# First stage in a written order, score banks for layer 1, context squares on two engines, adaLN rows a step behind, and common buffers for the spatial weights

## The chip, the core and the metric

The kernel runs on one core of a Trainium2 chip. A core has TensorE (PE) for matrix products, VectorE (DVE), ScalarE (ACT) and GpSimd (POOL) for everything else, SyncE (SP) that issues the DMA transfers, a software-managed SBUF and the accumulator memory PSUM. The metric is the time of one launch on the device in microseconds; smaller is better. Each engine runs its own list of instructions in order and waits at semaphores for the others.

## What is computed

A two-layer diffusion backbone. 512 latent tokens and 256 context tokens of width 1024 share the weights; layer 0 is a spatial-gating MLP beside differential attention, layer 1 multi-head latent attention. Each layer starts with an RMS norm whose scale and shift come from a conditioning vector (adaLN):

```python
def reference(x, c, ctx, c_ctx, ...):
    h_lat, h_ctx = x, ctx
    for li in range(DEPTH):
        shift_l, scale_l, gate_l = adaln_terms(c, ada_w[li], ada_b[li])      # silu(c) @ w_ada + b_ada
        shift_c, scale_c, gate_c = adaln_terms(c_ctx, ada_w[li], ada_b[li])
        xl = rms_norm(h_lat, norm_w[li]) * (1.0 + scale_l[:, None, :]) + shift_l[:, None, :]
        xc = rms_norm(h_ctx, norm_w[li]) * (1.0 + scale_c) + shift_c
        out_l, out_c = even_mixer(xl, xc, ...) if li % 2 == 0 else odd_mixer(xl, xc, ...)
        h_lat = h_lat + gate_l[:, None, :] * out_l
        if li < DEPTH - 1:
            h_ctx = h_ctx + gate_c * out_c
    return rms_norm(h_lat, final_w)

def spatial_gating(u, v, w_s, b_s, ln_w, ln_b):       # half of even_mixer
    vn = layer_norm(v, ln_w, ln_b)
    vc = vn.reshape(bsz, length // 128, 128, 8, 64)
    mixed = jnp.einsum('gpq,bnqgd->bnpgd', w_s, vc) + b_s.T[None, None, :, :, None]
    return u * mixed.reshape(bsz, length, 512)
```

## The kernel before

The 768 tokens are six tiles of 128: tiles 0 to 3 are latent, 4 and 5 context. The width of 1024 is cut into four quarters of two slices of 128. Every float32 operand of a product is split into a high part (ACT rounds it, `wh` or `xh`) and a low part (a subtraction, `wl` or `xl`), and a product is three matmuls (`mm3`, L79 to L81): high by high, low by high, high by low. Weights come by `load_w`: SP loads 512 KB into one of two `raw` buffers (tile `wr`), ACT makes `wh` (L66), DVE or POOL subtracts (`wl`, L67); the results lie in three common buffers each, or in a stage's own pool, where they are named `wo` (eight buffers in pool `p_a`). PSUM has eight banks: two `mm`, two `tr` for transposes, and two `S` tiles of two banks each for attention scores, which the first stage uses as accumulators, so that its six (`avb`) are two `mm` and four `S` banks.

The order of instructions on each engine is set by the Tile framework's own scheduler from the order in the program, priorities and dependences; `tc.issue_after` holds instructions back until another is issued, and `in_order(engines)` fixes the written order of those engines.

The places that the change touches:

- First stage (L169 to L436). DVE and ACT square the tokens (`ssq_vector`, tile `jk`, L345; `ssq_quarter`, tile `junk`, L228), `rstd_of` gives 1/rms (POOL, L155), `normalise` scales the tokens in place on ACT (L362). `ada_chunk(0, 0)` multiplies the conditioning vector by one 512-column chunk of adaLN weights on PE (32 small matmuls in four groups, L175, with three idling matmuls `turn_over` (L399) between the groups), copies the row out of PSUM (`arow`, L183), transposes it (L185), and adds biases (`AD`, `gT`, L192 to L195). `modulate_in` transposes a quarter's slice (L371), writes `xh` on ACT (L374), `xm` on DVE (L376) and `xl` as their difference (L379). `av_part` then runs the first projection over the quarters as they come, first four tiles of latents, then the two of context. Chunk 1 of the adaLN (L175 again) follows in the same stage.
- adaLN in the later stages: `ada_step` is called between the groups of matmuls of a projection and does one `ada_chunk`, with the row copied by ACT (L181).
- Spatial stage (L479 to L487): the weights `wsT` are split into `p_a`'s `wo` buffers, as are those of the az columns behind it. For each of eight groups PE makes three matmuls into an `mm` bank, and DVE evicts it (tile `au`, L486). Next come the az columns (az0, az1), then the query and key columns (q0, k0, ...), whose weights use the common buffers.
- Output projection of layer 0 and input of layer 1: the weights `owa` (four chunks of 448 columns) are split with the subtraction on POOL.
- Layer 1: `rows_done` transposes K' (L778) and the rotary key (L782) through `tr` banks; `latent_queries` accumulates in an `mm` bank; `odd_out` makes the output columns of each token tile in `mm` banks, adds them to the residual (`y` L1009, `xr` L1010), squares on ACT (L1012) and multiplies by the final weight (`yt`, L1013), on POOL for the first two quarters. After the last quarter of a tile `rstd_of` (L232, L234, POOL L155) and a scaling end it.

Of the kernel before, what the change touches and what calls it, by code (L numbers as in the profile page):

```python
# [30 lines left out]
def tile_backbone(ctx: ExitStack, tc: tile.TileContext, a: dict, out: bass.AP):  # L31
# [137 lines left out]
    def ada_chunk(li, j, ws, between=None, copy=None):  # L169


        ps = tr_ps()
        for kt in range(8):
            for b in range(4):
                PE.matmul(ps[32 * b:32 * b + 32, :P], c32[:, kt, :], ws[kt // 2][:, kt % 2, b * P:(b + 1) * P],  # L175
                          start=kt == 0, stop=kt == 7)
            if between and kt % 2:
                between(3)
        row = til(p_bg, [P, P], F32, "arow", 2)
        if copy is ACT:  # L180
            ACT.activation(row, ps[:, :P], AF.Copy)  # L181
        else:
            DVE.tensor_copy(row, ps[:, :P])  # L183
        ps = tr_ps()
        PE.transpose(ps[:, :P], row, ident)  # L185
        r = ps[:, :P].rearrange("p (b v) -> p b v", b=4)[:, :, :2]

        def wide(x):
            n = x.shape[1]
            return x.unsqueeze(2).to_broadcast([P, n, 2])  # L190
        if j < 4:
            DVE.tensor_tensor(AD[:, li, j, :2, :], r[:, :2], wide(adab[:, li, j, :2]), op=ALU.add)  # L192
# [16 lines left out]

    def ada_step():  # L210
# [141 lines left out]
    marks = []  # L352
    rs = [rstd_of(acc, 0, 4, marks)]
    POOL.tensor_scalar(adab1, adab[:, :, :4, 2:], 1.0, None, op0=ALU.add)
    with tc.issue_after(marks[1]):
        ws_in = [split_w(w0)]

    def normalise(j, v):
        t0, n = ((0, 4), (4, 2))[v]
        for t in range(n):  # L360
            x_ = xq[j][:, t0 + t, :]
            ACT.activation(x_, x_, AF.Copy, scale=rs[v][:, t:t + 1])  # L362

    def modulate_in(j, v, i, xh, xl):
# [4 lines left out]
        ps = tr_ps()[:, :n * P]  # L369
        for t in range(n):  # L370
            PE.transpose(ps[:, t * P:(t + 1) * P], xq[j][:, t0 + t, i * P:(i + 1) * P], ident)  # L371
# [24 lines left out]
    def turn_over(n):  # L396

        for _ in range(n):
            PE.matmul(avb[5][:, :P], ident, ident, start=True, stop=True)  # L399
# [8 lines left out]


    turn_over(32)  # L410
    normalise(0, 0)
    ada_chunk(0, 0, adaw[0], between=turn_over)
    for i in range(2):
        h = modulate_in(0, 0, i, *XT[0])
    turn_over(4)
    with tc.issue_after(h.ins):
        for q in range(4):
            ssq_quarter(xq[q], acc, q, 4, 1)
            ssq_vector(q, 5)
        rs.append(rstd_of(acc, 4, 2))  # L420
        normalise(0, 1)
    for i in range(2):
        modulate_in(0, 1, i, *XT[0])
    for j in range(4):
        if j < 3:
            with tc.issue_after(h.ins):
                for v in range(2):
                    normalise(j + 1, v)
        w = [x.rearrange("p (k n) -> p k n", k=2) for x in ws_in[j]]
        av_part(j, w, range(4))  # L430
# [48 lines left out]
    wsh, wsl = (x.rearrange("p (g n) -> p g n", g=8) for x in load_w(a["wsT"], p_a, 8))  # L479
# [207 lines left out]
    for c in range(4):  # L687
# [3 lines left out]
        split(raw, h, l, eng=POOL)  # L691
# [49 lines left out]
    def rows_done(v):  # L741
# [34 lines left out]
        ps = tr_ps()  # L776
# [3 lines left out]
        ps = tr_ps()  # L780
# [94 lines left out]
    def latent_queries(h):  # L875
        ps = mm_ps()
# [121 lines left out]
    def odd_out(j, w, ts):  # L998
        c = slice(j * 256, (j + 1) * 256)
        for t in ts:  # L1000
            ps = mm_ps()[:, :256]
# [11 lines left out]
            (POOL if j < 2 else DVE).tensor_tensor(yt[t][:, c], x_, finw[:, c], op=ALU.mult)  # L1013
# [101 lines left out]
```

## Time and profile before

| | |
|---|---|
| median of three runs | 712.65 us (711.88 to 713.12) |
| profiled execution, its own time | 712.08 us |
| span of the profiled execution | 710.3 us |
| mean granted TensorE clock | 0.992 of full speed |
| PE busy | 692.3 us (97%) |
| DVE / ACT / POOL busy | 441.2 (62%) / 363.1 (51%) / 42.8 us (6%) |
| DMA | 68.89 MB, mean 97 GB/s |

The span is from the first to the last recorded instruction; the profiled execution's own time is 1.8 us longer. An engine counts as busy while one of its instructions runs, not while it waits. "Idle before" in a row of the timeline is the engine's idle time just ahead of the instruction, and the name behind the arrow is what it waited for last.

### The profile page before, as it was taken

How to read it: one execution, taken by the hardware profiler on the slowest of the kernel's cores; microseconds unless marked ns; L12 is line 12 of the kernel's file. 1: busy time of each engine (PE TensorE's matmuls, PEld its weight loads, DVE VectorE, ACT ScalarE, POOL GpSimd, SP SyncE). 2: the span in 40 equal slices, each digit the busy share in tenths (PEclk: the TensorE clock that was granted, in tenths of full speed). 3: DMA queues.
4: the chain of work that ended last, by engine and by line, in shares of the span. 5: the costliest groups of instructions: out<-in, count | busy, mean ns of one | idle time of the engine just before them, and what ended most of it. 6: DMA issues, size and time to landing. Idle time of an engine off the chain costs nothing.

```text
span 710.3 us, 12674 instructions
## 1 busy us (share of the span) xinstructions
PE 692.3 (97%) x5260; PEld 637.4 (90%) x5260; DVE 441.2 (62%) x815; ACT 363.1 (51%) x704; POOL 42.8 (6%) x45
## 2 busy tenths in 40 slices
PE   8899999999999999999999999999999999999996
PEld 7688997998998989889899999978789999999995
DVE  2556814205397883979685327676448898876754
ACT  4756223214366763666543314444348777887422
POOL 1000000121001000010000300110000000000110
PEclk9999999999999999999999999999999999999998
DMA  9944893301111011110513310150210212011402
GB/s 340 408 135 154 327 352 134 119 1 31 37 54 41 20 60 42 38 41 1 230 44 117 102 30 1 60 202 31 95 60 0 69 59 83 30 60 30 119 31 90
DMA packets 20075, 68.89 MB, mean 97 GB/s; under 512 B 3121, under 2 KB 3249, under 8 KB 20017
## 3 DMA queue, kind: packets, MB, share of 16 engines
q1 hardware_dynamic: 20016, 68.08, 27.1%
q8 instruction: 41, 0.67, 0.4%
q14 instruction: 18, 0.14, 0.1%
HBM read 65.98 MB, written 2.10 MB: 96 GB/s over the span
## 4 chain that ended last, share of the span: by engine, by line
PE 82%; DVE 7%; DMA 5%; ACT 4%; issue 1%; POOL 1%; SPq 0%; POOLq 0%; ACTq 0%
PE mm L79 18%; PE mm L81 17%; PE mm L80 17%; PE S L79 3%; PE S L80 3%; PE S L81 3%; PE tr L925 3%; DMA x<-in_x 2%; PE S L565 2%; PE S L567 2%; PE tr L583 2%; PE tr L175 1%; PE S L903 1%; PE S L907 1%; DMA wr<-in_wsT 1%
## 5 line engine op out<-in xcount | busy, mean ns | idle before, releaser
L80 PE MATMUL mm<-xl,wh 128*128 128x512 f32 (+1 forms) x240 | 84.8, 354 | 0.0
L81 PE MATMUL mm<-xh,wl 128*128 128x512 f32 (+1 forms) x240 | 84.3, 351 | 0.0
L79 PE MATMUL mm<-xh,wh 128*128 128x512 f32 (+1 forms) x240 | 84.2, 351 | 0.0
L333 ACT ACTIVATE e<-S,s 128x768 f32<-128x768 f32 (+1 forms) x80 | 65.3, 817 | 17.5 <-DVE s L332 17.1
L66 ACT ACTIVATE wh<-wr 128x1024 fp32r<-128x1024 f32 (+1 forms) x40 | 41.8, 1049 | 54.4 <-PE mm L80 21.3
L67 DVE TENSOR_TENSOR wl<-wr,wh 128x1024 fp32r<-128x1024 f32 x36 | 44.5, 1238 | 40.4 <-ACT wh L66 40.4
L332 DVE TENSOR_REDUCE s<-S 128x1 f32<-128x768 f32 (+1 forms) x80 | 67.2, 841 | 3.7 <-PE S L907 1.8
L66 ACT ACTIVATE ah<-tr 128x512 fp32r<-128x512 f32 x76 | 43.9, 596 | 24.7 <-PE tr L583 12.6
L67 DVE TENSOR_TENSOR al<-tr,ah 128x512 fp32r<-128x512 f32 x76 | 50.3, 684 | 7.8 <-ACT ah L66 6.7
L80 PE MATMUL mm<-wl,xh 128*128 128x256 f32 (+1 forms) x176 | 51.4, 292 | 0.5 <-POOL wl L67 0.5
L79 PE MATMUL mm<-wh,xh 128*128 128x256 f32 (+1 forms) x176 | 51.5, 292 | 0.0
L81 PE MATMUL mm<-wh,xl 128*128 128x256 f32 (+1 forms) x176 | 50.8, 290 | 0.0
L79 PEld LDWEIGHTS mm<-xh,wh 128*128 128x128 f32 x240 | 45.2, 188 | 5.2 <-ACT wh L66 0.2
L80 PEld LDWEIGHTS mm<-xl,wh 128*128 128x128 f32 x240 | 45.2, 188 | 4.8
L81 PEld LDWEIGHTS mm<-xh,wl 128*128 128x128 f32 x240 | 45.2, 188 | 4.7
L79 PE MATMUL mm<-wo,xh 128*128 128x256 f32 x144 | 41.2, 286 | 2.1 <-DVE au L486 2.1
L80 PE MATMUL mm<-wo,xh 128*128 128x256 f32 x144 | 40.9, 284 | 0.0
L81 PE MATMUL mm<-wo,xl 128*128 128x256 f32 x144 | 40.7, 283 | 0.0
L155 POOL TENSOR_TENSOR s<-s,mhalf 128x6 f32<-128x6 f32 (+4 forms) x15 | 16.0, 1072 | 309.8 <-DVE s L605 179.3
L80 PEld LDWEIGHTS mm<-wl,xh 128*128 128x128 f32 x176 | 33.3, 189 | 1.2 <-POOL wl L67 0.7
L79 PEld LDWEIGHTS mm<-wh,xh 128*128 128x128 f32 x176 | 33.3, 189 | 0.9 <-issue 0.4
L81 PEld LDWEIGHTS mm<-wh,xl 128*128 128x128 f32 x176 | 33.1, 188 | 0.8
(283 smaller groups left out, 2007.8 us busy)
## 6 DMA issues: line engine op xcount, KB each, us to landing
ada<-in_ada SPq DMA_DIRECT2D x40, 512.0 KB, 7.3
wr<-in_ew SPq DMA_DIRECT2D x28, 512.0 KB, 3.5
wr<-in_ewo SPq DMA_DIRECT2D x8, 512.0 KB, 3.5
wr<-in_owz SPq DMA_DIRECT2D x8, 512.0 KB, 3.5
wr<-in_adr SPq DMA_DIRECT2D x8, 512.0 KB, 3.4
wr<-in_owo SPq DMA_DIRECT2D x8, 512.0 KB, 3.7
xr<-in_x SPq DMA_DIRECT2D x4, 768.0 KB, 6.5
x<-in_x SPq DMA_DIRECT2D x4, 512.0 KB, 4.8
```

Of the source, the lines that this page charges most:

```text
L66: ACT.activation(h, src, AF.Copy)
L67: (eng or DVE).tensor_tensor(l, src, h.bitcast(F32), op=ALU.subtract)
L79: PE.matmul(ps, lh, rh, start=first, stop=False)
L80: PE.matmul(ps, lh, rl, start=False, stop=False)
L81: PE.matmul(ps, ll, rh, start=False, stop=last)
L155: return POOL.tensor_tensor(dst, src, mhalf[:, :n], op=ALU.pow)
L332: mx = DVE.tensor_reduce(nmx[:, :1], v[:, :, :w], axis=AX.XY, op=ALU.max, negate=True)
L333: ACT.activation(e.rearrange("p (c k) -> p c k", k=w), v[:, :, :w], AF.Exp, bias=nmx[:, :1], scale=1.0, accum_out=sm[:, col:col + 1])
L565: PE.matmul(S[:, c, :n], QS[:, m, qs], KS[:, m, k0:k0 + n], start=True, stop=False)
L567: scored = PE.matmul(S[:, c, :n], QS[:, m, qs], KL[:, m, k0:k0 + n], start=False, stop=True)
L583: PE.transpose(ps[:, i * 256 + q * P:i * 256 + (q + 1) * P], es[q][:, (2 * j + i) * P:(2 * j + i + 1) * P], ident)
L925: PE.transpose(ps[:, i * 256 + q * P:i * 256 + (q + 1) * P], es[q][:, (2 * j + i) * P:(2 * j + i + 1) * P], ident)
```

## The change

1. First stage. ACT, DVE and PE run in written order from `normalise(0, 0)` to the first context rows. Behind the first two groups of ada products stand two idling matmuls each, behind the third and fourth the transposes of the first quarter's two slices (into an idle accumulator bank and a `tr` bank). The first weight chunk `w0` is split inside this order: `wh` on ACT before `xh`, `wl` on DVE between the first slice's `xm` and its `xl`. The row copy `arow` stands on DVE right behind the products. Of the eight context squares ACT makes five and DVE three, where each made four. `av_first` runs the first quarter's 24 latent matmuls in three passes, high by high, low weights, low tokens.
2. `ada_chunk` is cut into `ada_products` and `ada_rows`; `ada_step` first transposes the row of the step before, then makes its own products.
3. `wsT` goes to the common `wh` and `wl` buffers.
4. `owa`'s subtractions move from POOL to DVE. K' and the rotary key are transposed into the two banks of an `S` tile, the first head's latent query goes into an `S` bank, and `odd_out` alternates between `mm` and `S` banks.
5. The final weight's multiply is on DVE for all quarters; three of the four sums of squares are added and scaled before the last quarter, and the fourth is added by one instruction behind it.

The diff, cut to its core:

```diff
-    def ada_chunk(li, j, ws, between=None, copy=None):
+    def ada_products(ws, between=None, copy=None):
...
             if between and kt % 2:
-                between(3)
+                between(kt)
...
+    def ada_rows(li, j, row):
         ps = tr_ps()
         PE.transpose(ps[:, :P], row, ident)
...
     def ada_step():
+        if ada_row:
+            ada_rows(*ada_row.pop())
         if ada_done[0] < len(ada_rest):
-            ada_chunk(*ada_loaded[ada_done[0]], copy=ACT)
+            li, j, ws = ada_loaded[ada_done[0]]
+            ada_row.append((li, j, ada_products(ws, copy=ACT)))
...
+    def av_first(w, ts):
+        (xh, xl), (wh, wl) = XT[0], w
+        for n, (x_, w_) in enumerate(((xh, wh), (xh, wl), (xl, wh))):
+            for i in range(2):
+                for t in ts:
+                    PE.matmul(avb[t], x_[:, i, t * P:(t + 1) * P], w_[:, i, :], start=n + i == 0, stop=False)
...
     turn_over(32)
-    normalise(0, 0)
-    ada_chunk(0, 0, adaw[0], between=turn_over)
-    for i in range(2):
-        h = modulate_in(0, 0, i, *XT[0])
-    turn_over(4)
-    with tc.issue_after(h.ins):
+    with in_order(ACT, DVE, PE):
+        normalise(0, 0)
+        xt0 = []
+        def fill_in(kt):
+            if kt < 5:
+                turn_over(2)
+            else:
+                i = len(xt0)
+                xt0.append(turned(0, 0, i, tr_ps() if i else avb[4]))
+        ada_chunk(0, 0, adaw[0], between=fill_in)
+        ACT.activation(w0h, w0, AF.Copy)
+        turn_over(6)
+        modulate_in(0, 0, 0, *XT[0], ps=xt0[0],
+                    between=lambda: DVE.tensor_tensor(w0l, w0, w0h.bitcast(F32), op=ALU.subtract))
+        for q in range(1, 4):
+            ssq_vector(q, 5)
+        modulate_in(0, 0, 1, *XT[0], ps=xt0[1])
         for q in range(4):
-            ssq_quarter(xq[q], acc, q, 4, 1)
-            ssq_vector(q, 5)
+            ssq_quarter(xq[q], acc, q, 4, 1 if q else 2)
         rs.append(rstd_of(acc, 4, 2))
-        normalise(0, 1)
+        normalise(1, 0)
+        h = normalise(0, 1)
+    av_first(w, range(4))
...
-    wsh, wsl = (x.rearrange("p (g n) -> p g n", g=8) for x in load_w(a["wsT"], p_a, 8))
+    wsh, wsl = (x.rearrange("p (g n) -> p g n", g=8) for x in load_w(a["wsT"]))
...
-        split(raw, h, l, eng=POOL)
+        split(raw, h, l)
...
-        ps = tr_ps()
+        S = ps_s.tile([P, 2, 512], F32, tag="S", name=nm("S"))
+        ps = S[:, 0, :]
...
-        ps = tr_ps()
+        ps = S[:, 1, :]
...
-        ps = mm_ps()
+        ps = mm_ps() if h else ps_s.tile([P, 2, 512], F32, tag="S", name=nm("S"))[:, 0, :]
...
-            ps = mm_ps()[:, :256]
+            ps = (mm_ps() if t % 2 else ps_s.tile([P, 2, 512], F32, tag="S", name=nm("S"))[:, 0, :])[:, :256]
...
-            (POOL if j < 2 else DVE).tensor_tensor(yt[t][:, c], x_, finw[:, c], op=ALU.mult)
+            DVE.tensor_tensor(yt[t][:, c], x_, finw[:, c], op=ALU.mult)
...
-        rs = rstd_of(acc, t, 1)
+        DVE.tensor_reduce(part[:, :1], acc[:, t * 4:t * 4 + 3], axis=AX.X, op=ALU.add)
+        DVE.tensor_scalar(part[:, :1], part[:, :1], 1.0 / D, 1e-6, op0=ALU.mult, op1=ALU.add)
+        odd_out(3, wo[2], (t,))
+        DVE.scalar_tensor_tensor(ms[:, :1], acc[:, t * 4 + 3:t * 4 + 4], 1.0 / D, part[:, :1], op0=ALU.mult, op1=ALU.add)
+        rsqrt(rs[:, :1], ms[:, :1], 1)
```

Where this puts the instructions is seen in the engines' lists. DVE in the first stage, before, from the first context square to the first `xm` (x_96 to x_99 are the quarters of the tokens, tr and S are PSUM banks, wr_116 is the raw chunk `w0`):

```order
L345 SCALAR_TENSOR_TENSOR jk_311,s_144<-x_96 128x256
L67 TENSOR_TENSOR wl_184<-wr_116,wh_183 128x1024
L345 SCALAR_TENSOR_TENSOR jk_315,s_144<-x_97 128x256
L345 SCALAR_TENSOR_TENSOR jk_319,s_144<-x_98 128x256
L345 SCALAR_TENSOR_TENSOR jk_323,s_144<-x_99 128x256
L183 COPY arow_280<-tr_235 128x128
L192 TENSOR_TENSOR AD<-tr_282,adab_sb 128x4
L194 TENSOR_TENSOR gT<-tr_282,adab_143 128x4
L195 TENSOR_TENSOR gT<-gT,normw_sb 128x4
L376 TENSOR_SCALAR xm_292<-tr_287,gT,AD 128x512
```

The same place in the changed kernel:

```order
L182 COPY arow_279<-tr_233 128x128
L195 TENSOR_TENSOR AD<-tr_281,adab_sb 128x4
L197 TENSOR_TENSOR gT<-tr_281,adab_143 128x4
L198 TENSOR_TENSOR gT<-gT,normw_sb 128x4
L392 TENSOR_SCALAR xm_293<-S_186,gT,AD 128x512
L452 TENSOR_TENSOR wl_196<-wr_116,wh_195 128x1024
L397 TENSOR_TENSOR xl_39_188<-xm_293,xh_38_187 128x512
L357 SCALAR_TENSOR_TENSOR jk_298,s_144<-x_97 128x256
L357 SCALAR_TENSOR_TENSOR jk_300,s_144<-x_98 128x256
L357 SCALAR_TENSOR_TENSOR jk_302,s_144<-x_99 128x256
L392 TENSOR_SCALAR xm_304<-tr_274,gT,AD 128x512
L397 TENSOR_TENSOR xl_39_188<-xm_304,xh_38_187 128x512
```

The row copy and what hangs on it now stand ahead of the squares and of `wl`, and `wl` stands between the first slice's `xm` and `xl`.

PE in the first stage, before, from the third group of ada products to the first matmuls of the projection:

```order
L175 MATMUL tr_235<-ada_112,c_14_138 32x128 x8
L399 MATMUL S_190<-ident 128x128 x3
L175 MATMUL tr_235<-ada_114,c_14_138 32x128 x8
L399 MATMUL S_190<-ident 128x128 x3
L185 MATMUL tr_282<-ident,arow_280 128x128
L371 MATMUL tr_287<-ident,x_96 128x128 x4
L371 MATMUL tr_296<-ident,x_96 128x128 x4
L399 MATMUL S_190<-ident 128x128 x4
L79 MATMUL mm_187<-wh_183,xh_40_191 128x512
L80 MATMUL mm_187<-wl_184,xh_40_191 128x512
L79 MATMUL mm_188<-wh_183,xh_40_191 128x512
L80 MATMUL mm_188<-wl_184,xh_40_191 128x512
```

The same place in the changed kernel:

```order
L174 MATMUL tr_233<-ada_112,c_14_138 32x128 x8
L378 MATMUL S_186<-ident,x_96 128x128 x4
L174 MATMUL tr_233<-ada_114,c_14_138 32x128 x8
L378 MATMUL tr_274<-ident,x_96 128x128 x4
L188 MATMUL tr_281<-ident,arow_279 128x128
L417 MATMUL S_185<-ident 128x128 x6
L433 MATMUL mm_183<-wh_195,xh_38_187 128x512
L433 MATMUL mm_184<-wh_195,xh_38_187 128x512
L433 MATMUL S_185<-wh_195,xh_38_187 128x512 x2
L433 MATMUL mm_183<-wh_195,xh_38_187 128x512
L433 MATMUL mm_184<-wh_195,xh_38_187 128x512
L433 MATMUL S_185<-wh_195,xh_38_187 128x512 x2
```

The token transposes moved ahead of the row's transpose, two of the idling groups became those transposes, and the high weights come for all four tiles before the low ones.

DVE in the spatial stage, before, from the fourth eviction (`au`) to the weights behind the last (wl_1858 is q0's, wo_1673 az1's, wl_1932 k0's):

```order
L486 SCALAR_TENSOR_TENSOR au_856<-mm_1471,absT_sb,au_856 128x6x64
L486 SCALAR_TENSOR_TENSOR au_857<-mm_1476,absT_sb,au_857 128x6x64
L486 SCALAR_TENSOR_TENSOR au_857<-mm_1481,absT_sb,au_857 128x6x64
L67 TENSOR_TENSOR wl_1858<-wr_1855,wh_1857 128x1024
L486 SCALAR_TENSOR_TENSOR au_857<-mm_1486,absT_sb,au_857 128x6x64
L486 SCALAR_TENSOR_TENSOR au_857<-mm_1491,absT_sb,au_857 128x6x64
L67 TENSOR_TENSOR wo_1673<-wr_1670,wo_1672 128x1024
L67 TENSOR_TENSOR wl_1932<-wr_1929,wh_1931 128x1024
```

The same place in the changed kernel (wl_1851 is q0's, wl_1925 k0's):

```order
L530 SCALAR_TENSOR_TENSOR au_849<-mm_1459,absT_sb,au_849 128x6x64
L198 TENSOR_TENSOR gT<-gT,normw_sb 128x4
L67 TENSOR_TENSOR wl_1851<-wr_1848,wh_1850 128x1024
L530 SCALAR_TENSOR_TENSOR au_850<-mm_1464,absT_sb,au_850 128x6x64
L530 SCALAR_TENSOR_TENSOR au_850<-mm_1469,absT_sb,au_850 128x6x64
L67 TENSOR_TENSOR wl_1925<-wr_1922,wh_1924 128x1024
L530 SCALAR_TENSOR_TENSOR au_850<-mm_1474,absT_sb,au_850 128x6x64
L530 SCALAR_TENSOR_TENSOR au_850<-mm_1479,absT_sb,au_850 128x6x64
L67 TENSOR_TENSOR wl_1995<-wr_1992,wh_1994 128x1024
```

q0's subtraction moved from ahead of the last two evictions to ahead of the last four, k0's from behind the last eviction to ahead of the last two, and az1's is gone from here: it stands ahead of the first eviction.

## Rows read from the trace of the kernel before

**Rows 1.** which engines are busy over the whole span (the page's first part)

```profile
PE 692.3 (97%) x5260; PEld 637.4 (90%) x5260; DVE 441.2 (62%) x815; ACT 363.1 (51%) x704; POOL 42.8 (6%) x45
```

**Rows 2.** what PE waited for: us in total, times, longest us

```profile
PE tr L185 <- DVE arow L183: 3.4, 1, 3.4
PE mm L79 <- DVE au L486: 2.1, 1, 2.1
...
PE tr L778 <- DVE cql L70: 0.8, 1, 0.8
PE mm L79 <- ACT z L870: 0.7, 1, 0.7
PE mm L80 <- POOL wl L67: 0.5, 1, 0.5
...
PE mm L79 <- DVE y L1009: 0.3, 1, 0.3
PE tr L185 <- ACT arow L181: 0.3, 1, 0.3
```

**Rows 3.** timeline of the first stage: start us, us, instruction, [idle before <-releaser]

```profile
15.22 1.06 ACT L66 ACTIVATE wh<-wr 128x1024 fp32r<-128x1024 f32 x1 [2.26 <-DMA wr<-in_ew]
...
15.84 0.94 PE L399 MATMUL S<-ident 128*128 128x128 f32 x6
...
17.28 0.42 DVE L345 SCALAR_TENSOR_TENSOR jk<-x 128x256 f32<-128x256 f32 x1 [7.19 <-DMA x<-in_x]
...
17.64 1.22 DVE L67 TENSOR_TENSOR wl<-wr,wh 128x1024 fp32r<-128x1024 f32 x1
...
19.81 0.28 DVE L183 COPY arow<-tr 128x128 f32<-128x128 f32 x1
...
20.93 0.16 DVE L195 TENSOR_TENSOR gT<-gT,normw_sb 128x4 f32<-128x4 f32 x1
21.52 1.63 ACT L374 ACTIVATE xh<-tr,AD,gT 128x512 fp32r<-128x512 f32 x2 [5.24 <-PE tr L371]
...
22.33 1.66 DVE L376 TENSOR_SCALAR xm<-tr,gT,AD 128x512 f32<-128x512 f32 x2 [1.24 <-ACT xh L374]
...
23.32 0.48 PE L79 MATMUL mm<-wh,xh 128*128 128x512 f32 x1
...
23.91 1.28 DVE L379 TENSOR_TENSOR xl<-xm,xh 128x512 fp32r<-128x512 f32 x2
...
25.50 0.63 PE L81 MATMUL mm<-wh,xl 128*128 128x512 f32 x2
...
29.95 1.96 PE L175 MATMUL tr<-ada,c 128*32 128x128 f32 x64
...
32.46 0.28 DVE L183 COPY arow<-tr 128x128 f32<-128x128 f32 x1
```

**Rows 4.** stretch, its us, busy (x) of PE PEld DVE ACT POOL, PEclk, DMA share, GB/s

```profile
20.00:24.00 4.00, 3.85 (x20) 3.76 (x21) 2.12 (x7) 2.41 (x7) 0.00 (x0) 0.63 1.03 411
120.00:124.90 4.90, 2.70 (x12) 1.75 (x12) 3.46 (x6) 2.00 (x2) 0.00 (x0) 1.00 0.16 63
124.90:129.00 4.10, 4.07 (x21) 4.07 (x22) 1.83 (x3) 1.06 (x1) 0.00 (x0) 0.58 0.67 227
```

**Rows 5.** timeline of the spatial stage, columns as in rows 3

```profile
116.05 1.22 DVE L67 TENSOR_TENSOR wo<-wr,wo 128x1024 fp32r<-128x1024 f32 x1 [0.18 <-ACT wo L66]
...
122.03 1.06 ACT L66 ACTIVATE wh<-wr 128x1024 fp32r<-128x1024 f32 x1 [4.71 <-DMA wr<-in_ew]
...
123.12 1.23 DVE L67 TENSOR_TENSOR wl<-wr,wh 128x1024 fp32r<-128x1024 f32 x1 [1.15 <-ACT wh L66]
```

**Rows 6.** loads of `wr` in the first 140 us, issue to landing

```profile
DMA to landing us min/median/max: 3.3/4.1/10.2
```

**Rows 7.** timeline of layer 1's input stage

```profile
460.22 2.12 POOL L67 TENSOR_TENSOR wl<-wr,wh 128x896 fp32r<-128x896 f32 x1 [13.59 <-ACT wh L66]
```

**Rows 8.** timeline of the tail

```profile
704.86 0.16 DVE L232 TENSOR_REDUCE s<-s 128x1 f32<-128x4 f32 x1 [0.17 <-ACT junk L1012]
```

More of the change, by code (lines that the diff above doesn't have):

```diff
@@ L183, in ada_chunk @@
             DVE.tensor_copy(row, ps[:, :P])
+        return row
+    def ada_rows(li, j, row):
         ps = tr_ps()
@@ L197, in ada_chunk @@
             DVE.tensor_tensor(AD[:, li, j, :, :], r, wide(adab[:, li, j, :]), op=ALU.add)
+    def ada_chunk(li, j, ws, between=None):
+        ada_rows(li, j, ada_products(ws, between))
     ada_rest = [(0, 4), (0, 5)] + [(1, j) for j in range(4)]
@@ L361, in normalise, with turned, modulate_in @@
             x_ = xq[j][:, t0 + t, :]
-            ACT.activation(x_, x_, AF.Copy, scale=rs[v][:, t:t + 1])
-    def modulate_in(j, v, i, xh, xl):
+            i = ACT.activation(x_, x_, AF.Copy, scale=rs[v][:, t:t + 1])
+        return i
+    def turned(j, v, i, ps):
+        t0, n = ((0, 4), (4, 2))[v]
+        for t in range(n):
+            PE.transpose(ps[:, t * P:(t + 1) * P], xq[j][:, t0 + t, i * P:(i + 1) * P], ident)
+        return ps[:, :n * P]
+    def modulate_in(j, v, i, xh, xl, ps=None, between=None):
         t0, n = ((0, 4), (4, 2))[v]
@@ L368, in modulate_in @@
         kt = 2 * j + i
-        ps = tr_ps()[:, :n * P]
-        for t in range(n):
-            PE.transpose(ps[:, t * P:(t + 1) * P], xq[j][:, t0 + t, i * P:(i + 1) * P], ident)
+        if ps is None:
+            ps = turned(j, v, i, tr_ps())
         m = til(p_in, [P, NL], F32, "xm", 2)[:, :n * P]
@@ L378, in modulate_in @@
             ACT.activation(m, ps, AF.Identity, bias=shift_of(0, kt, v), scale=g)
+        if between:
+            between()
         DVE.tensor_tensor(xl[:, i, cols], m, xh[:, i, cols].bitcast(F32), op=ALU.subtract)
@@ L398, in turn_over @@
         for _ in range(n):
-            PE.matmul(avb[5][:, :P], ident, ident, start=True, stop=True)
+            PE.matmul(avb[3][:, :P], ident, ident, start=True, stop=True)
     def av_part(j, w, ts):
@@ L427, in tile_backbone @@
                 for v in range(2):
-                    normalise(j + 1, v)
+                    if j + v:
+                        normalise(j + 1, v)
         w = [x.rearrange("p (k n) -> p k n", k=2) for x in ws_in[j]]
-        av_part(j, w, range(4))
+        if j > 0:
+            av_part(j, w, range(4))
         if j < 3:
@@ L1019, in tile_backbone @@
     for t in range(4):
-        for j in (2, 3):
-            odd_out(j, wo[j - 1], (t,))
-        rs = rstd_of(acc, t, 1)
+        odd_out(2, wo[1], (t,))
+        part = small(8)
+        DVE.tensor_reduce(part[:, :1], acc[:, t * 4:t * 4 + 3], axis=AX.X, op=ALU.add)
+        DVE.tensor_scalar(part[:, :1], part[:, :1], 1.0 / D, 1e-6, op0=ALU.mult, op1=ALU.add)
+        odd_out(3, wo[2], (t,))
+        ms, rs = small(8), small(8)
+        DVE.scalar_tensor_tensor(ms[:, :1], acc[:, t * 4 + 3:t * 4 + 4], 1.0 / D, part[:, :1], op0=ALU.mult, op1=ALU.add)
+        rsqrt(rs[:, :1], ms[:, :1], 1)
         DVE.tensor_scalar(yt[t][:, :640], yt[t][:, :640], rs[:, :1], None, op0=ALU.mult)
```

9 lines of the change are left out of this document (5 added, 4 removed).

## The prediction

> **What bounds the kernel now.** I read the page's first part first. PE is busy 692.3 of 710.3 us [rows 1], so only 18 us of the span are not TensorE work, and a change that leaves the arithmetic alone can win no more than a part of those 18. Next I read who waited for whom on PE [rows 2]: one wait of 3.4 us at the start (L185 for the copy `arow`), one of 2.1 us in the spatial stage (L79 for the eviction `au`), then 0.8, 0.7, 0.5, 0.3 and 0.3. The rest of the 18 is the start before the first load lands, the tail after the last matmul, and gaps too short for the view. Last I read the timeline of the stretches round these waits [rows 3, 5] and the granted clock behind the two long ones [rows 4]: TensorE was granted 0.63 between 20 and 24 us and 0.58 between 124.9 and 129 us, a mean of its two levels of 1.2 and 2.4 GHz, each time right after one of these two waits. So a long wait costs twice: itself, and about 4.0 x 0.37 = 1.5 us or 4.1 x 0.42 = 1.7 us of slower matmuls.
>
> **First stage.** In the timeline [rows 3] the fourth group of ada products is done at 15.84, when three idling matmuls (six passes, 0.94 us with their drain, about 0.29 each) follow, as they did behind the other three groups. But DVE copies the row (`arow`) only at 19.81, since a context square (17.28, whose data have just come), the subtraction `wl` (17.64, 1.22 us) and three more squares stand ahead of it. PE waits those 3.4 us, and its first real matmul starts at 23.32.
>
> By hand for the changed kernel. The first two fill-ins lose one matmul each (0.29), and the third, now four transposes instead of three matmuls (0.86), is put at 0.6, so the products end at about 15.84 - 0.58 - 0.26 = 15.0 and `arow` starts there: nothing stands ahead of it on DVE any more. From `arow` to gT are 1.3 us before (19.81 to 20.93 and its 0.16), so gT is there at 16.3. That is also when ACT ends `wh` of w0 (15.22 and 1.06). xh follows at 0.8 each (1.63 for two): 16.3 to 17.1 to 17.9. The first real matmul is at about 17.3, 6 us earlier than before. It can't all be kept, because DVE becomes the late engine: xm 0.83, `wl` 1.22, xl 0.64, three squares at 0.36 (17.28 to 17.64), xm 0.83, xl 0.64, together 5.2 us from 17.2, so the second xl is there at 22.4. The 24 matmuls of `av_first` take 5.6 us at 0.235 (two of them 0.63 at 25.50, with one drain of 0.16); xl is wanted by the last eight, the second xl at 22.0; they end at 23.3. Then the context's rstd, its normalise and four transposes come, about 1.3 us of PE waiting in two pieces, and the products of chunk 1 start at about 25.9 against 29.95. By then PE has done 26 of the chunk's 36 matmuls instead of 24. The gain is 4.05 + 2 x 0.235 = **4.5**. The row copy after these products gives a check: DVE reaches it at about 29.3 instead of 32.46, 3.1 us earlier, with six matmuls more behind it (1.4): 4.5 again. Bounds: if xm waits for xh again as it did at 22.33 (1.24), once in each of the two pairs, 2.5 of it go and 2.0 stays; with no wait at all for the context 1.3 more comes, 5.8. I keep 4.5, since each duration in it is a row of this stretch. Three of the four context squares stay on DVE and ACT gets one more; ACT stood idle 5.24 us before its xh (row at 21.52), which hides that.
>
> **Spatial stage.** The 2.1 us wait comes from DVE: q0's weights land at 122.03 (ACT idle 4.71 for the DMA), ACT splits, DVE's `wl` runs 123.12 to 124.35 [rows 5], and the last two evictions stand behind it in DVE's order. The change puts the spatial weights in the common buffers, so that az1's two splits come one slot earlier, and q0's load goes out when the first of them is done (about 115.9) and k0's when the second is (117.27, as the second subtraction of this stretch, 116.05 and 1.22, ends there before). k0's load thus takes the very slot of q0's load before, and DVE's order has its `wl` ahead of the last two evictions as q0's was, and q0's `wl` ahead of the two before those. PE should wait about 1.2 us at the fifth group's eviction and 1.4 at the seventh's, and az1 starts at about 124.9 on the old clock: **0**, the stall is cut in two and not removed. Bounds: q0's own stall can vanish if it lands early (the shortest load in this part took 3.3 us [rows 6], for which DVE would be done with the fourth eviction anyway): no gain, since k0's comes after. The slower matmuls behind the stall (1.7) either stay or vanish. I let them stay, because PE's idle time in the stage is the same in sum.
>
> The Trainium skill, "TensorE: Matmul & The Clock Gate", section "A second HAM failure mode: psum-queue depth-cycling", reports a kernel in which short pauses of PE between matmul groups, while banks are cycled, were enough for the clock to swing. That rule speaks against this change: by it the two shorter stalls cost the same 1.7 (the forecast); were only long waits to count, the time would be 1.7 lower (rival A). The rows here show a fall behind the waits of 3.4 and 2.1 only, so they don't decide.
>
> **adaLN rows one step behind.** PE's wait for the row copied by ACT is 0.3 [rows 2]; the transposes go behind the next step's products, where the row is long ready. One group of DVE's small instructions moves with it, a step later, and its consumers are stages away. **0.3.**
>
> **Layer 1.** Three waits of [rows 2] lose their cause. (a) L80 for POOL's `wl`, 0.5: the subtraction took POOL 2.12 us [rows 7]; on DVE, by the 1.23 us of 1024 columns [rows 5], 896 take about 1.1. `wh` is ready at about 460.2, so DVE would be done at 461.3, before PE wants it at 461.9. Three other subtractions go to DVE in the output stage of layer 0, 3 x 1.1 us, where DVE waits for PE's results several times per block; I cost them at nothing, and at 3.3 if that cover were gone. (b) L778 for cql, 0.8: the wait is for a tr bank, and K' now goes into a score bank. (c) L79 for z, 0.7: the same with an mm bank and the first latent query. Together **2.0**. Bounds: 0, if the next bank is late instead (score banks hold the low-rank results until DVE has copied them), and 2.0.
>
> **Output.** The wait for `y` (0.3) [rows 2] goes with four banks for two: **0.3**. The multiplies of two quarters move from POOL to DVE, off the path while PE has banks. In the tail the sum over four columns (0.16, [rows 8]) and the scaling behind it become one instruction after the last square, so one of two goes, with the step between them: **0.2**.
>
> **Sum.** 4.5 + 0 + 0.3 + 2.0 + 0.3 + 0.2 = 7.3 us off the profiled execution: 712.1 - 7.3 = 704.8 (span 703.0; 1.8 lie outside the span). That execution is 0.6 under the median of the runs, so the forecast against the median of 712.65 is **705.4**.
>
> **Rivals.**
> - A: the clock no longer falls in the spatial stage, because neither stall is as long as the waits of 3.4 and 2.1: 705.4 - 1.7 = **703.7**. For it: all rows of a lower clock stand behind longer waits. Against: two stalls 2 us apart. 0.18.
> - B: the first stage gives part back. PE now has pauses of 0.7 before the first matmul and twice 0.7 at the context's rows, and the clock may fall there as it did at 20 us (1.5 us by [rows 4]), or DVE's chain is later by the 1.24 of the row at 22.33 once or twice. 1.5 to 2.5: **707.4**. 0.20. By the section of the Trainium skill named above, short pauses would do for such a fall; no row of the kernel before shows one.
> - C: the bank changes of layer 1 don't do what they say: the score banks are held and PE waits as long as before, 705.4 + 2.0 = 707.4; together with B, 709.4. 0.12.
> - D, slower: the weights of q0 and k0 land late, and the evictions stand behind both subtractions. Each us of landing beyond the usual is a us of PE, twice. With the median landing of 4.1 and the longest of 10.2 [rows 6], two late loads cost up to 2 x 6.1 = 12.2: **717.6**. It decides from the point where the two are late by 7.3 + 1.4 together, that is each lands at 8.5 or later. Against it: between 120 and 124.9 the DMA engines were 0.16 busy [rows 4], so nothing crowds these loads. 0.04.
>
> **How the numbers follow.** Forecast 0.46, A 0.18, B 0.20, C 0.12, D 0.04. About 0.2% (1.4 us) is what a measurement of this kernel can tell from no change, so "same" is 711.2 to 714.1. Forecast, A, B and C alone lie below 711.2. Of the 0.32 of B and C I give 0.06 to both coming together with the 3.3 us of POOL's work on DVE's path, which is 712.7; of D 0.01 ends around no change and 0.03 above, and 0.02 more of slower is for C with B at a larger price: faster 0.88, same 0.07, slower 0.05. The range goes from A with 1 us of the start's upper bound (702.7) to B with C (709.4).
>
> **What would show it.** In the changed kernel's trace: no wait of PE for `arow` in the first 20 us; the first real matmul at 17.3, chunk 1's products at 25.9, and a granted clock near 1 from 17 to 24 us (B otherwise). In the spatial stage two waits for `au` of 1.2 and 1.4, 4.5 us earlier on the clock of the trace than 124.9, and a granted clock of about 0.6 for 4 us behind them (A otherwise). No waits for POOL's `wl`, cql or z, and no new ones named S or `cr` in their place (C otherwise). The tail from the last matmul to the end 0.2 shorter than 7.0. The prediction is wrong if DVE, at 62% before and with POOL's subtractions added, shows up as releaser of PE in places where it didn't before.

## The result

| | kernel before | changed kernel |
|---|---|---|
| median, all runs of the first comparison | 712.88 us (711.88 to 716.27, four runs) | 702.25 us (702.14 to 704.46, four runs) |
| profiled execution, its span | 712.08, 710.3 us | 702.23, 700.1 us |
| mean granted TensorE clock | 0.992 | 0.998 |
| PE busy | 692.3 us (97%) | 687.0 us (98%) |
| DVE / ACT / POOL busy | 441.2 / 363.1 / 42.8 us | 445.6 / 363.3 / 28.0 us |

The ratio is 0.985, 95% interval 0.981 to 0.989: 10.6 us faster where 7.3 were forecast, 0.45 us below the lower end of the range. When both were run again beside b1 to b4 (below), the same program has 701.95 (700.5 to 704.1) and the kernel before 714.19 (710.9 to 717.4): 12.2 us.

The page's first part of the changed kernel, and who waited for whom on PE (us in total, times, longest), to set beside [rows 1, 2]:

```profile
PE 687.0 (98%) x5248; PEld 633.1 (90%) x5248; DVE 445.6 (64%) x829; ACT 363.3 (52%) x706; POOL 28.0 (4%) x33
```

```profile
PE mm L79 <- DVE au L530: 2.5, 3, 1.3
...
PE S L79 <- ACT xh L390: 0.5, 1, 0.5
...
PE tr L378 <- ACT x L371: 0.4, 1, 0.4
PE mm L433 <- ACT xh L390: 0.2, 1, 0.2
```

The waits for `arow`, cql, z, POOL's `wl` and `y` are gone; the wait for `au` is in pieces and no shorter (2.5 us for 2.1). To see where the 10 us come from I took the same matmul in both timelines and subtracted its start times. This lead of the changed kernel grows as follows; b1 is a second profile of the same program.

| place in the program | lead, first profile | lead, b1 | grows by (first profile) | forecast |
|---|---|---|---|---|
| last matmul of the first stage | 4.65 | 3.91 | 4.65 | 4.5 |
| first matmul of the spatial stage | 5.67 | 5.70 | 1.02 | 0.3 |
| first matmul behind its stalls | 5.76 | 5.88 | 0.09 | 0 |
| end of the az columns, 34 us later | 6.11 | 5.88 | 0.35 | 0 |
| end of layer 0's output | 6.00 | 6.08 | -0.11 | 0 |
| scores of layer 1 begin | 8.88 | 8.88 | 2.88 | 2.0 |
| last matmul of the attention | 9.29 | 9.24 | 0.41 | 0 |
| last matmul of the output | 9.99 | 9.64 | 0.70 | 0.3 |
| end of the span | 10.2 | 9.9 | 0.2 | 0.2 |

So no step that was forecast went the wrong way; most of the small ones gave more. The 0.41 of the attention is not the change's: d1 (below), which changes nothing there, gains 0.40 in it too. The timeline of the changed kernel's first stage (start us, us, instruction, [idle before <-releaser]), to set beside [rows 3]:

```profile
14.77 0.29 DVE L182 COPY arow<-tr 128x128 f32<-128x128 f32 x1 [4.72 <-PE tr L174]
...
16.94 0.81 DVE L392 TENSOR_SCALAR xm<-S,gT,AD 128x512 f32<-128x512 f32 x1 [1.03 <-ACT xh L390]
16.96 0.73 PE L433 MATMUL mm<-wh,xh 128*128 128x512 f32 x2 [0.17 <-ACT xh L390]
...
21.28 0.69 DVE L397 TENSOR_TENSOR xl<-xm,xh 128x512 fp32r<-128x512 f32 x1
...
23.63 0.84 PE L378 MATMUL tr<-ident,x 128*128 128x128 f32 x4 [0.40 <-ACT x L371]
...
25.01 0.50 PE L79 MATMUL S<-wh,xh 128*128 128x512 f32 x1 [0.55 <-ACT xh L390]
...
25.68 1.95 PE L174 MATMUL tr<-ada,c 128*32 128x128 f32 x64
...
28.85 0.28 DVE L182 COPY arow<-tr 128x128 f32<-128x128 f32 x1
```

The hand walk had `arow` at 15.0, the first real matmul at 17.3, the second xl ready at 22.4 (21.97 here), two waits at the context's rows, chunk 1's products at 25.9 and its row copy at 29.3: each within 0.5 us. (The adaLN products start 0.48 us earlier than in the kernel before, 10.46 and 10.94; more on that under the reasons below.) The granted clock is 1.00 from 17 to 24 us.

The spatial stage, beside [rows 5]:

```profile
114.70 1.23 DVE L67 TENSOR_TENSOR wl<-wr,wh 128x1024 fp32r<-128x1024 f32 x1
...
116.51 0.45 PE L79 MATMUL mm<-vnh,wh 128*128 128x384 f32 x1 [1.00 <-DVE au L530]
...
117.37 1.22 DVE L67 TENSOR_TENSOR wl<-wr,wh 128x1024 fp32r<-128x1024 f32 x1 [0.39 <-ACT wh L66]
...
119.17 0.39 PE L79 MATMUL mm<-wo,xh 128*128 128x256 f32 x1 [1.34 <-DVE au L530]
```

Two waits of 1.00 and 1.34 stand where 1.2 and 1.4 were foreseen, each behind a `wl`.

### The profile page after: what moved, and what is told of

The parts are those of the page before. It is cut to its first block, busy times and chain, and to the rows that moved or that the text cites. A ratio compares the mean times of both kernels' runs of the same rounds, so it can differ in the third digit from the quotient of the medians.

```text
span 700.1 us, 12647 instructions
## 1 busy us (share of the span) xinstructions
PE 687.0 (98%) x5248; PEld 633.1 (90%) x5248; DVE 445.6 (64%) x829; ACT 363.3 (52%) x706; POOL 28.0 (4%) x33
## 4 chain that ended last, share of the span: by engine, by line
PE 89%; DVE 4%; ACT 3%; DMA 3%; issue 0%; SPq 0%; POOL 0%; POOLq 0%; ACTq 0%
PE mm L79 19%; PE mm L80 18%; PE mm L81 18%; PE S L79 4%; PE S L81 4%; PE S L80 4%; PE tr L970 3%; PE tr L174 2%; PE S L609 2%; PE S L611 2%; DMA wr<-in_ew 2%; PE tr L627 2%; PE S L948 1%; PE S L952 1%; PE tr L79 1%; PE tr L644 1%
## 5 line engine op out<-in xcount | busy, mean ns | idle before, releaser
L67 DVE TENSOR_TENSOR wl<-wr,wh 128x1024 fp32r<-128x1024 f32 (+1 forms) x40 | 48.3, 1209 | 42.5 <-ACT wh L66 40.9
L79 PE MATMUL mm<-wh,xh 128*128 128x256 f32 (+1 forms) x172 | 49.7, 289 | 0.0
L80 PE MATMUL mm<-wl,xh 128*128 128x256 f32 (+1 forms) x172 | 49.5, 288 | 0.0
L81 PE MATMUL mm<-wh,xl 128*128 128x256 f32 (+1 forms) x172 | 49.0, 287 | 0.0
```

The costliest lines, as they stand in the source:

```text
L67: (eng or DVE).tensor_tensor(l, src, h.bitcast(F32), op=ALU.subtract)
L79: PE.matmul(ps, lh, rh, start=first, stop=False)
L80: PE.matmul(ps, lh, rl, start=False, stop=False)
L81: PE.matmul(ps, ll, rh, start=False, stop=last)
```

## The experiments

A lead is always that over the first profile of the kernel before, at the same matmul.

**First part alone, and three parts taken out, one at a time.** a1 is the kernel before with only the ordered first stage:

> The kernel before with the ordered first stage alone; everything else as before. The changed kernel's trace is 4.65 us ahead of the kernel before at the end of the first stage (and up to 5.3 inside it). Theory T1 (the parts add up, each saves what the ladder of the two traces shows at its place): 712.9 - 4.65 = 708.2, with the spatial stall of 2.1 us and the slow clock behind it still there. Theory T2 (the first stage also brings loads and splits forward, so that later waits shrink): below 707.5. Theory T3 (the lead is partly given back at the next wait for a load): above 709.5.

Measured: 708.0 us (706.4 to 711.1) beside 712.96 for the kernel before in this comparison, 5.0 us less. Its lead is 4.58 at the end of the first stage, 4.23 at the spatial stage, 4.34 behind the az columns and 4.11 at the last matmul. T1: the first stage is worth 4.6 and gives nothing to the rest; it even loses 0.35 on the way to the spatial stage, where PE waits 1.2 for a row `arow` instead of 0.3.

a2 puts the spatial weights back:

```diff
-    wsh, wsl = (... for x in load_w(a["wsT"]))
+    wsh, wsl = (... for x in load_w(a["wsT"], p_a, 8))
```

> The changed kernel with the spatial weights back in the stage's own buffers; all else changed. One stall of about 2.1 us should be back before az1, with the granted clock at about 0.6 for 4 us. T1 (the fall of the clock costs 1.7 us, but matmuls of 256 columns then run 0.1133 us apart instead of 0.1177 for the next 40 us, which gives 1.35 back): 702.3 + 0.4 = 702.7. T2 (the clock alone counts): 702.3 + 1.7 = 704.0. T3 (the buffers also brought loads of the stages before forward, 0.5 us between 69 and 93 us): 0.5 more than either.

Measured: 700.7 us (699.8 to 703.7), less than the changed kernel, which none of the three expected. Its longest stall is 1.4, not 2.1, and in its profile no fall of the clock came back. Its lead behind the az columns is 8.65. But a3 has the changed kernel's own program up to layer 0's output and stands at 8.34 there, against 6.11 in the changed kernel's profile. So a difference of this size needs no cause in the weights' buffers; it is there between two executions of one program, and b1 and b2 were made to see that.

a3 undoes everything in layer 1 (subtractions on POOL, tr and mm banks, the output, the tail):

> The changed kernel with the owa subtractions back on POOL, the tr and mm banks of layer 1 back, the output on mm banks alone, two yt quarters on POOL and the old end of the tail. T1 (ladder: 2.9 us from 460 to 518 us, 0.4 to 646, 0.7 in the output, 0.2 in the tail): 702.3 + 4.2 = 706.5. T2 (the named waits and the tail only: 2.0 + 0.3 + 0.2): 702.3 + 2.5 = 704.8.

Measured: 704.5 us (704.0 to 705.3), 2.3 above the changed kernel's first median, which is T2's number. But place by place it is T1: from layer 0's output to the scores of layer 1 the lead falls by 0.26 instead of growing by 2.88, and in the output it falls by 0.15 instead of growing by 0.70. The 2.2 us that a3 was ahead before those places hide half of the difference in the totals.

a4 transposes each adaLN row in its own step again:

```diff
     def ada_step():
-        if ada_row:
-            ada_rows(*ada_row.pop())
         if ada_done[0] < len(ada_rest):
             li, j, ws = ada_loaded[ada_done[0]]
-            ada_row.append((li, j, ada_products(ws, copy=ACT)))
+            ada_rows(li, j, ada_products(ws, copy=ACT))
```

> The changed kernel with each adaLN row transposed in its own step again. T1 (ladder: the lead grows by 1.0 us between the first stage and the spatial stage): 703.3. T2 (the named wait of 0.3 only): 702.6. T3 (the lead there comes from the weights' buffers and not from the rows): 702.3.

Measured: 705.0 us (703.2 to 707.2), more than any of the three. The lead at the spatial stage is 3.91 against 5.67, 1.76 less. (The two profiles end 2.05 apart, so only 0.3 comes behind the spatial stage, although the clock fell there in a4's profile: a4 then ran the az columns at 0.1133 us a matmul, the changed kernel's profile at 0.1177.) The timeline of a4 shows what the row waits for:

```profile
89.34 1.06 ACT L66 ACTIVATE wh<-wr 128x1024 fp32r<-128x1024 f32 x1 [2.33 <-DMA wr<-in_wsT]
90.30 0.26 ACT L180 ACTIVATE arow<-tr 128x128 f32<-128x128 f32 x1
...
90.62 0.33 PE L188 MATMUL tr<-ident,arow 128*128 128x128 f32 x1 [1.01 <-ACT arow L180]
```

On ACT the row's copy stands behind the split of the spatial weights, and that waits for its load. In the kernel before this wait of PE was 0.3 [rows 2]. PE is 4.6 us earlier by then; the split of the spatial weights, at 89.34 instead of 93.25, only 3.9. So the wait is 1.0 here and 1.2 in a1. In the changed kernel the same copy comes at 90.10, and PE takes the row a step later, at 93.40, without a wait.

**The part on rows alone.** d1 is the kernel before with that part only:

> The kernel before with the adaLN rows transposed one step behind, alone. Taken out of the changed kernel this part cost 2.8 us of the median and 1.8 us of the lead at the spatial stage, six times the 0.3 that the trace of before shows. T1 (the wait grows only when the first stage is early: in a4_rows_same_step ACT's row copy stands behind a split that waits for a load, and the load isn't earlier while PE is): alone the part brings 0.3 to 0.5 us at the start of the spatial stage. T2 (the part is worth 1.8 us by itself): 1.5 or more there.

Measured: one run of 707.7 beside 711.7. Its lead grows by 1.77 from the end of the first stage (0.74) to the spatial stage (2.51), T2's number; but its 256-column matmuls between 76 and 112 us are 0.1136 us apart (their pitch, from start to start) and those of the kernel before 0.1177, which, added up matmul by matmul, makes 0.9 of it. About 0.9 is left for the part, between T1 and T2. In the kernel before PE waits for such a row twice in that stretch, the first time too shortly for the view of waits (0.10):

```profile
77.26 0.28 PE L79 MATMUL mm<-wh,xh 128*128 128x256 f32 x1
77.64 0.33 PE L185 MATMUL tr<-ident,arow 128*128 128x128 f32 x1
77.72 0.36 PE L80 MATMUL mm<-wl,xh 128*128 128x256 f32 x1
```

```profile
93.97 0.28 PE L79 MATMUL mm<-wo,xh 128*128 128x256 f32 x1
94.53 0.33 PE L185 MATMUL tr<-ident,arow 128*128 128x128 f32 x1 [0.28 <-ACT arow L181]
94.61 0.36 PE L80 MATMUL mm<-wo,xh 128*128 128x256 f32 x1
```

A matmul and a transpose take 0.46 and 0.64 us here; without a wait they are 0.118 and 0.11, so the two waits cost about 0.23 and 0.41, most of the 0.9. In the changed kernel's first profile the lead grows by 1.02 in this stretch, 0.18 of it pitch: 0.84, about the same as alone. Taken out of the changed kernel the part costs more, 1.76 less 0.18 of pitch, about 1.6, because the wait that comes back is the 1.0 of a4 and not 0.3.

**The same programs once more, and two that take the subtractions out of DVE's way.**

> The changed kernel once more, beside the next three, to learn how far its runs lie apart. The first comparison gave 702.1 to 704.5. In its profile nearly all matmuls of 256 columns between 72 and 153 us are 0.1177 us apart, in a3_layer1_old, whose program is the same up to there, 0.1135. Theory T1 (which of the two pitches a stretch runs at differs from run to run): the runs spread over 2 to 4 us, the profile shows other stretches at the short pitch, median 702 to 703.5. T2 (the pitch belongs to the program): the same stretches at the same pitch, spread under 1 us.

Measured: 701.95 us (700.5 to 704.1), a spread of 3.6. T1: two executions of one program run the same matmuls at two pitches. The same twelve matmuls in the timelines of the two profiles show it:

```profile
89.27 0.28 PE L80 MATMUL mm<-wo,xh 128*128 128x256 f32 x1
...
90.69 0.28 PE L80 MATMUL mm<-wo,xh 128*128 128x256 f32 x1
```

```profile
89.79 0.28 PE L80 MATMUL mm<-wo,xh 128*128 128x256 f32 x1
...
91.15 0.28 PE L80 MATMUL mm<-wo,xh 128*128 128x256 f32 x1
```

The first is the changed kernel's first profile, 1.42 / 12 = 0.118; the second is b1, 1.36 / 12 = 0.113. In b1 the clock also fell behind the spatial stage, in the first profile not. Two stretches of each (stretch, its us, busy time and count of PE, PEld, DVE, ACT, POOL, granted clock, DMA share, GB/s), the first profile above, b1 below:

```profile
119.00:121.00 2.00, 1.82 (x15) 1.83 (x16) 0.96 (x3) 1.39 (x2) 0.00 (x0) 1.00 0.66 221
121.00:123.00 2.00, 2.00 (x19) 2.00 (x19) 0.91 (x1) 0.95 (x1) 0.00 (x0) 1.00 0.19 57
```

```profile
119.00:121.00 2.00, 1.95 (x10) 1.95 (x11) 0.79 (x2) 1.34 (x2) 0.00 (x0) 0.59 0.65 248
121.00:123.00 2.00, 2.00 (x12) 2.00 (x12) 0.96 (x1) 1.00 (x1) 0.00 (x0) 0.55 0.06 23
```

The stalls ahead of them are alike (1.00 and 1.34; 1.11 and 1.14).

> The kernel of a2_spatial_own (spatial weights in the stage's own buffers, all else changed) once more, beside the changed kernel. T1 (the buffers are worth nothing, the 1.5 us between the two medians came from pitch and clock): within 1 us of the changed kernel's median. T2 (the common buffers cost time, since they put two subtractions ahead of evictions instead of one): 1 to 2 us below it. T3 (they gain): 1 us above.

Measured: 701.8 us (700.7 to 703.4) beside b1's 701.95. T1: where the spatial weights lie makes no difference that these runs, each spread over some 3 us, can tell.

b3 takes the cause of the two stalls away; b4 does the same to a2, for q0 alone:

```diff
-        pl, pc = proj_feat(XT, load_w(wch[16 + 2 * h]), SPANS)
+        pl, pc = proj_feat(XT, load_w(wch[16 + 2 * h], eng=POOL if h == 0 else DVE), SPANS)
```

> The changed kernel with the subtractions of q0's and k0's weights on POOL, so that none stands ahead of the last four evictions on DVE. T1 (the stalls of 1.0 and 1.3 us are DVE's order alone): no wait of PE for au over 0.3, 2.3 us less than the changed kernel, no fall of the clock in any run there. T2 (POOL's subtractions of 2.1 us slow DVE's evictions beside them or come late for q0): under 1 us less.

> The kernel of a2_spatial_own with q0's subtraction on POOL. T1: its stall of 1.4 us goes, 1.4 us below b2_spatial_own_again and about where b3_qk_on_pool is. T2 (the last two evictions then wait for something else, the late az1 weights): no difference.

Measured: b3 699.1 us (698.3 to 701.1), 2.9 below b1; b4 700.4 (698.8 to 701.3), 1.4 below b2. T1 for both, except that b4 is 1.3 above b3 and not level with it. In b3's profile the lead grows by 1.99 from the spatial stage's first matmul to the first behind it, in b1's by 0.18. PE's waits and POOL's subtraction in b3:

```profile
PE mm L79 <- DVE au L530: 0.6, 3, 0.3
```

```profile
115.17 2.40 POOL L67 TENSOR_TENSOR wl<-wr,wh 128x1024 fp32r<-128x1024 f32 x1 [45.41 <-ACT wh L66]
115.46 1.14 DVE L530 SCALAR_TENSOR_TENSOR au<-mm,absT_sb,au 128x384 f32<-128x384 f32 x2 [0.36 <-PE mm L81]
```

POOL needs 2.4 us where DVE needs 1.2, but nobody waits for it, and the two evictions beside it take 1.14 together, as two do in the changed kernel. In the profiles of b3 and b4 the clock did not fall behind this stage. b3 is faster than both kernels.

**Layer 1 and the output, piece by piece.** Each is the changed kernel with two or three pieces undone at places far apart, one profile each, read against the first profile of the changed kernel. Each was run once, beside 711.7 for the kernel before: c1 705.0, c2 702.2, c3 705.8.

> The changed kernel with owa's subtractions back on POOL and the output on mm banks alone; read place by place against the changed kernel. T1 (the lead gained between the end of layer 0's output and the end of the 448-column products, 0.76 us, is POOL's late wl; that of the output, 0.7, is the banks): 0.7 to 0.8 less lead at the first place and 0.6 to 0.7 less in the output. T2 (the named waits alone): 0.5 and 0.3.

Measured: with POOL's subtraction the lead from layer 0's output to the end of the 448-column products falls by 0.02 instead of growing by 0.76; the wait that is back:

```profile
PE mm L79 <- DVE y L1054: 0.5, 1, 0.5
PE mm L80 <- POOL wl L67: 0.5, 1, 0.5
```

In the output the lead falls by 0.26 instead of growing by 0.70, so the banks are worth 0.96 there. T1, or more.

> The changed kernel with K' and the rotary key in tr banks, two yt quarters on POOL, and the eight context squares shared four to four again. T1: between the first cr transpose and the scores of layer 1 the lead is 0.6 to 1.2 us smaller; yt changes nothing; the fourth square on DVE (0.36 us in its chain) costs 0.3 to 0.4 at the end of the first stage. T2 (ACT's fifth square delays the context as much as DVE's fourth did): no difference in the first stage.

Measured: from the first cr transpose to the query weights of layer 1 the lead grows by 0.35 instead of 1.15: K' in the score banks is worth 0.80, with a named wait of 0.5. In the output the lead grows as in the changed kernel (0.72 and 0.70), so yt's place is worth nothing there. (The tail of c2 is 0.65 longer, half of it a late last square on ACT and half the landing of the last output; whether yt on POOL has a part in that, one execution doesn't tell.) At the end of the first stage the lead is 4.05, c1 has 3.83 and c3, whose first stage like c1's is the changed kernel's, 4.03. But the first adaLN products start at different times, 11.44 in c1, 11.24 in c3 and 10.77 in c2, so the stage has to be counted from there. c1 above, c2 below:

```profile
11.44 0.64 PE L174 MATMUL tr<-ada,c 128*32 128x128 f32 x16
...
24.48 0.84 PE L378 MATMUL tr<-ident,x 128*128 128x128 f32 x4 [0.40 <-ACT x L371]
```

```profile
10.77 0.65 PE L174 MATMUL tr<-ada,c 128*32 128x128 f32 x16
...
22.55 0.73 PE L433 MATMUL mm<-wh,xl 128*128 128x512 f32 x2 [0.38 <-DVE xl L397]
...
24.15 0.84 PE L378 MATMUL tr<-ident,x 128*128 128x128 f32 x4 [0.41 <-ACT x L371]
```

From the first product to the context's transposes are 13.04 us in c1 and c3 and 13.38 in c2, to the end of the stage 53.67 and 54.12. T1: the fourth square on DVE makes PE wait 0.4 for xl, and the context is that much later.

> The changed kernel with the first latent query in an mm bank and the old end of the tail. T1: about 1.0 us less lead where the scores of layer 1 begin (the 0.7 of the named wait and small gaps behind it) and 0.2 us more from the last matmul to the end. T2 (the named wait alone): 0.7; tail 0.

Measured: from the query weights to the scores the lead grows by 0.00 instead of 0.97; from the start of the last matmul to the end are 7.3 us instead of 7.0. T1 for both. Its total is 3.6 above the changed kernel: the clock fell behind its spatial stage, and for longer (0.50 to 0.53 from 119 to 125 us). Over the az columns it loses 1.1 on the kernel before where a3, c2 and d1, at the same pitch and with the clock up, gain 1.6: 2.7 lost.

## Why the prediction was wrong, point by point

The direction and the mechanism of each part were right, the first stage within 0.5 us; what failed is the price that the sum gave to a removed wait of PE. The forecast 705.4 was 3.2 us too high, with the range ending 0.45 above the measured time. The misses of the steps in the two profiles add up: 0.15 + 0.72 + 0.09 + 0.35 - 0.11 + 0.88 + 0.41 + 0.40 = 2.9, the 10.2 that were gained less the 7.3 that were forecast.

**First stage, 4.5 forecast.** 4.65 in the first profile and 4.6 in a1; 3.5 to 4.1 in b1 to b4 and c1 to c3, where the first adaLN products start later (at 10.46 in the first profile, 11.36 in b1, 11.72 in b3). They don't wait for their weights, which land at 10.03, 10.60 and 10.35; they stand behind the 64 passes of idling matmuls at the start of the program, and those take longer. The changed kernel's first profile above, b3 below:

```profile
1.57 8.97 PE L417 MATMUL S<-ident 128*128 128x128 f32 x64 [1.57 <-POOL ident masks.py:199]
```

```profile
1.57 10.22 PE L417 MATMUL S<-ident 128*128 128x128 f32 x64 [1.57 <-POOL ident masks.py:199]
```

Until 4.90 us in the first profile, 5.94 in the kernel before and 7.49 in b3 they are 0.21 us apart, from there on 0.11; the granted clock is recorded as 1.00 all the while. This belongs to the execution and not to the change. Counted from the first product the lead is 4.2 in the first profile and 4.0 to 4.3 in all others with the changed first stage (3.9 in c2), so the step was right to 0.5, and the 4.65 is closer by luck. Part of it is the clock of the kernel before: d1 has the same first stage, kept 1.00, and is 0.6 ahead of it, counted the same way. Rival B did not happen: there are pauses, but the clock stays at 1.00. The step on context squares was right too: with the fourth on DVE PE is 0.35 to 0.45 later (c2).

**Layer 1, 2.0 forecast, and the output, 0.3: the step that failed most.** I took the price of a wait from the view of waits. That view counts from the end of the previous matmul's row, 0.28 us behind its start, while the next one starts 0.11 behind it when nothing waits; and it leaves out that the first matmul behind a wait is slow. The timeline of the kernel before shows both:

```profile
461.66 0.28 PE L79 MATMUL mm<-wh,xh 128*128 128x256 f32 x1
462.39 0.39 PE L80 MATMUL mm<-wl,xh 128*128 128x256 f32 x1 [0.45 <-POOL wl L67]
462.62 0.28 PE L81 MATMUL mm<-wh,xl 128*128 128x256 f32 x1
```

```profile
509.80 0.40 PE L81 MATMUL mm<-cqh,wl 128*128 128x512 f32 x1
510.89 0.50 PE L79 MATMUL mm<-cqh,wqkh 128*128 128x512 f32 x1 [0.69 <-ACT z L870]
511.23 0.39 PE L80 MATMUL mm<-cql,wqkh 128*128 128x512 f32 x1
```

From 461.66 to 462.62 are 0.96 us for two matmuls that take 2 x 0.113 when nothing waits: the wait of 0.45 costs 0.73. From 509.80 to 511.23 are 1.43 for 2 x 0.23: the wait of 0.69 costs 0.97. Taking the pieces out gave 0.78 (c1), 0.97 (c3) and 0.80 for a named 0.5 (c2). At a granted clock of 1.00 every wait of PE over 0.25 behind the first stage costs 0.26 to 0.28 more than its name ahead of a product, and 0.13 to 0.22 more ahead of a transpose, in the profiles of both kernels, a1, a3, b1, b3, c1 to c3 and d1. So the five removed waits of the sum, put at 0.8, 0.7, 0.5, 0.3 (`y`) and 0.3 (`arow`), cost 1.04, 0.96, 0.72, 0.55 and 0.41 from start to start, and the sum has 1.1 too little for them; with the short wait for a row that it didn't know, 1.3, nearly half of the whole miss. Of the rest, 0.44 is the pitch of the 256-column matmuls (0.18 in the step on rows, 0.26 in the attention) and 0.35 the clock, less what the pitch took back (below). Rival C, that the next bank is late instead, did not happen.

**Rows one step behind, 0.3 forecast.** 1.0 in the table of leads, 0.84 without the pitch. The step took one wait of two, and that by its name. It also left out what the first stage does to this place: PE is earlier, the load that ACT waits for ahead of the row's copy is not to the same degree, so without the part the wait would have grown to 1.0 (a4) or 1.2 (a1). The table doesn't show that, since it compares with the kernel before; a4 does, where the part is worth about 1.6.

**Spatial stage, 0 forecast.** Right in its place: two stalls for one, and b2 beside b1 shows no difference by the buffers. That the stalls are DVE's order was right too (b3).

**The clock, rival A.** It stayed up in the changed kernel's first profile, which is worth 1.6 (what a3, c2 and d1 gain on the kernel before over the az columns at the same pitch; the 1.7 of the prediction was right); it fell in b1, c1 and c3, whose program is the same up to there, and not in a3. So A was neither right nor wrong: both happen. Where it stayed up in the first profile, most of it was given back, because the next 34 us of matmuls ran at 0.1177 and those of the kernel before at 0.1133. The section of the Trainium skill that the prediction named ("TensorE: Matmul & The Clock Gate", "A second HAM failure mode: psum-queue depth-cycling") tells of a kernel in which frequent short pauses between matmul groups made the clock swing; b1 agrees, with stalls of 1.11 and 1.14 and 0.55 to 0.59 behind them, and c1 with a longest stall of 1.4. The first profile has stalls as long, 1.00 and 1.34, and no fall, which the section does not tell.

**Range.** It was too narrow below: its low end took rival A with 1 us of the first stage, and left no room for waits that cost more than their name. Its 0.2% for what a measurement can tell was too fine as well: the medians of the kernel before lie between 711.7 and 714.2, and one program's runs spread over 3.6 us. Faster, which had 0.88, was right.

What stays open: what decides between the two pitches and whether the clock falls, from one execution to the next.

## What to carry to other kernels

Price a wait of PE from start to start of the matmuls round it, not from the view of waits: here a wait cost 0.26 to 0.28 us more than its name ahead of a product and 0.13 to 0.22 ahead of a transpose. When one part of a change makes an engine several us earlier, read again each later wait for a load, since loads don't come earlier by as much; a part that looks worth 0.3 can be what keeps the others' gain. And compare two profiles place by place before totals: a3 and c3 have totals 2 us off what their edits do. Even then count a stage from its own first instruction: c2's lead at the end of the first stage hid 0.45.

## What the runs showed of the hardware that was not expected

- Matmuls of 256 columns run at one of two pitches at a granted clock of 1.00, 0.1133 and 0.1177 us, for stretches of up to 65 us; the pitch of a stretch differs between executions of one program (the twelve matmuls above). Of some 260 us of such matmuls per execution about 57 (the changed kernel's first profile) to 109 us (d1) were at the short one. Were all of them (about 150 to 204 us at the long one, 3.7% of it), the time would be some 5.5 to 7.5 us less, an estimate.
- The clock falls to 1.2 GHz behind a stall in some executions of a program and not in others. d1 waited 3.4 us for `arow`, as the kernel before does, and kept a clock of 1.00 from 20 to 24 us; there the kernel before had 0.63 [rows 4]. b2 kept it behind a stall of 1.9 us and d1 behind one of 2.2; in a1 it fell to 0.58 behind one of 2.0.
- At the start of the program the idling matmuls are 0.21 us apart, twice their later 0.11, until 4.5 to 7.5 us, by the execution, while the record of the granted clock reads 1.00: at a start, that record alone doesn't tell how fast TensorE runs.
